# Gate and up columns of a SwiGLU block as one 2x2 block product, three of eight k units with seven products in place of eight

## The chip, the cores and the metric

The kernel runs on one core of a Trainium2 chip. The metric is the device time of one execution in microseconds (us); lower is better. The engines that matter here are TensorE (PE in the profile; its weight loads are PEld), VectorE (DVE), ScalarE (ACT), GpSimd (POOL) and SyncE (SP, which issues the weight DMAs).

## The reference, cut to what matters

One decoder layer on 256 tokens of width 2048, in float32: a SwiGLU half-step, a mixer, and a second SwiGLU half-step with its own weights. The change touches the two SwiGLU steps alone, and in them the first two products:

```python
D_MODEL, SEQ, D_FF = 2048, 256, 5504

def swiglu(x, w_gate, w_up, w_down):
    return (jax.nn.silu(x @ w_gate) * (x @ w_up)) @ w_down

f1 = swiglu(rms_norm(h, ffn1_pre_norm[l]), ffn1_w_gate[l], ffn1_w_up[l], ffn1_w_down[l])
h = h + 0.5 * rms_norm(f1, ffn1_post_norm[l])
...
f2 = swiglu(rms_norm(h, ffn2_pre_norm[l]), ffn2_w_gate[l], ffn2_w_up[l], ffn2_w_down[l])
h = h + 0.5 * rms_norm(f2, ffn2_post_norm[l])
```

## The kernel before, in words

Every product of float32 matrices is made of three matmuls on TensorE. A number is split into a high part that fits TensorE's short float32 form (`F32R`) and the rest: `split_into` (L135) writes `hi` with a ScalarE copy (L136) and `lo = src - hi` with a VectorE subtract (L137). `mm3` (L139) then issues hi*hi, lo*hi and hi*lo into one PSUM bank (L141, L142, L143). The normed tokens are kept split and transposed as `xhi`, `xlo`; the weights are split as they arrive.

The 256 tokens are two row tiles t = 0, 1 of 128. The 2048 rows of a weight matrix are 16 k tiles of 128. `D_FF` = 5504 columns are worked in blocks of `CB` = 512: ten of 512 and a last one of 384. The loop over the blocks is in `ffn` (L380). For each block, `gemm_block` (L145) makes gate, then `gemm_block` makes up. A `gemm_block` walks the eight pairs of k tiles; this text calls such a pair a **unit**. For each unit, `wload` (L114) brings a `raw` tile of 128 x 2 x 512 with one DMA on SP's queue, `wchunk` (L121) splits it into `whi` and `wlo`, and twelve matmuls follow (two row tiles, two k tiles, three each). So a unit of gate and up together takes 24 matmuls, and a block of 512 columns takes 192. `raw`, `whi` and `wlo` are rings of `RING` = 5 tiles each: ScalarE may split a new tile only when TensorE has finished with the one five tiles earlier.

Behind a block, ScalarE applies silu to gate (L411), `finish` (L394) multiplies it with up on VectorE into `hn` (L396), and one step later TensorE transposes `hn` (four 128x128 transposes per row tile, L206) and ScalarE copies the result to `hT` (L401) for the down projection. Such later steps are generators: `side.spawn` starts one, and each `side.pump()` in a gemm lets each go one step. PSUM has eight banks of 128x512 float32, handed out from one pool by `ps_tile`.

The program's statements aren't the order in which an engine gets its instructions: a list scheduler with the tile pools sets it when the kernel is built, and each engine then works its list in order. Splits of a later unit are therefore found ahead of work of an earlier one.

`rows` is a pool of eight 128x512 tiles for the norm weights that `load_bcast` (L189) loads in `out_proj`; `hkhi` and `hklo` (four buffers each) hold the split `hT` in the down projection.

Of the kernel before, what the change touches and what calls it, by code (L numbers as in the profile page):

```python
# [74 lines left out]
def kernel(ctx: ExitStack, tc: tile.TileContext, a: dict, out: bass.AP):  # L75
# [69 lines left out]
    def gemm_block(w_dram, c0, w, lhs, nkt=KT, held=None, raws=(), ready=()):  # L145
# [40 lines left out]
        return pss if nb > 1 else [ps[0] for ps in pss]  # L186


    def load_bcast(name, n, after):  # L189
# [4 lines left out]
        return t

# [184 lines left out]
    def ffn(pre, x, rs, post, pre_next, begin=None, ready=(), following=None):  # L380
        with ExitStack() as fctx:
# [22 lines left out]
            for f0 in range(0, DFF, CB):  # L404
                w = min(CB, DFF - f0)
                g = gemm_block(a[pre + "_w_gate"], f0, w, xl, held=None if f0 or begin else held,
                               raws=() if f0 else raws, ready=() if f0 else ready)
                s = []
                for t in range(NT):
                    st = fwork.tile([P, CB], F32, tag="silu", name=nm("silu"))  # L410
                    nc.scalar.activation(st[:, :w], g[t][:, :w], AF.Silu, scale=rs[t])  # L411
# [483 lines left out]
```

## Time and profile before

| | |
|---|---|
| median of 3 runs | 2181.24 us (2180.39 to 2182.26) |
| the profiled execution, its own time | 2182.85 us |
| its span, first to last instruction | 2181.1 us |
| granted TensorE clock, mean | 0.999 |
| TensorE busy | 2170.1 us, 99% |
| VectorE busy | 1163.3 us, 53% |
| ScalarE busy | 997.8 us, 46% |
| HBM read | 406.41 MB, 187 GB/s over the span |

The span is the part of the execution that the trace sees; 1.75 us of the execution's own time lie around it. A matmul's record runs from its start to the modelled end of its results, about 0.39 us for 512 columns, and the next one starts before that; what a matmul costs in a stream is the distance between starts. Rows of instructions read: line, engine, operation, output<-inputs, shape, count, then busy time and the mean of one, then the idle time before them and what ended it.

### The profile page before, as it was taken

The numbers are of one execution on the slowest core, as the hardware profiler recorded it, in microseconds if no ns is written. First come the engines' busy times: TensorE is split into PE (matmuls) and PEld (weight loads), VectorE is DVE, ScalarE is ACT, GpSimd is POOL, SyncE is SP. The second block draws the span as 40 slices with busy tenths as digits, with TensorE's granted clock in tenths as the row PEclk, the third lists the DMA queues.
The fourth block names the chain that finished last, engine by engine and source line by source line (L and its number), as shares of the span: only waits on it lengthen the run. The fifth ranks groups of instructions, "written<-read, shape, count | busy, mean of one in ns | idle before, by whom it ended". The sixth has DMA issues, their size and how long they took to land.

```text
span 2181.1 us, 26346 instructions
## 1 busy us (share of the span) xinstructions
PE 2170.1 (99%) x10204; PEld 1815.8 (83%) x10204; DVE 1163.3 (53%) x1277; ACT 997.8 (46%) x1227; POOL 34.3 (2%) x87
## 2 busy tenths in 40 slices
PE   9999999999999999999999999999999999999998
PEld 7888888898888888888888888888888888898887
DVE  5544454445555744657575556575444444445555
ACT  6444444444445564444434444464444444444443
POOL 0000000000000100000000000010000000000000
PEclk9999999999999999999999999999999999999999
DMA  7666666667667456655556775756666666576663
GB/s 259 188 190 188 191 192 185 192 179 238 193 194 227 146 175 193 174 149 143 161 157 179 200 207 187 226 190 182 187 192 192 184 192 190 170 225 193 194 194 129
DMA packets 189360, 410.24 MB, mean 188 GB/s; under 512 B 13697, under 2 KB 22305, under 8 KB 189234
## 3 DMA queue, kind: packets, MB, share of 16 engines
q1 hardware_dynamic: 183440, 399.69, 61.5%
q10 hardware_dynamic: 5794, 8.87, 1.2%
q8 instruction: 80, 1.31, 0.2%
q14 instruction: 46, 0.38, 0.0%
HBM read 406.41 MB, written 2.10 MB: 187 GB/s over the span
## 4 chain that ended last, share of the span: by engine, by line
PE 99%; DVE 0%; DMA 0%; ACT 0%; issue 0%; DVEq 0%; POOLq 0%; SPq 0%; POOL 0%; ACTq 0%
PE mm L141 23%; PE mm L143 23%; PE mm L142 23%; PE acc L142 8%; PE acc L141 8%; PE acc L143 8%; PE ps L206 2%; PE ps L568 1%; PE ps L618 0%; PE ps L575 0%; PE ps L552 0%; DMA raw<-in_ffn_w_gate_dram 0%; PE ps L621 0%; PE ps L628 0%; DVE wlo L137 0%; DVE h L331 0%
## 5 line engine op out<-in xcount | busy, mean ns | idle before, releaser
L137 DVE TENSOR_TENSOR wlo<-raw,whi 128x1024 fp32r<-128x1024 f32 (+3 forms) x740 | 896.7, 1213 | 921.7 <-ACT whi L136 881.0
L136 ACT ACTIVATE whi<-raw 128x1024 fp32r<-128x1024 f32 (+3 forms) x740 | 777.0, 1051 | 1083.1 <-PE mm L142 808.0
L141 PE MATMUL mm<-whi,xhi 128*128 128x512 f32 (+2 forms) x2120 | 819.0, 387 | 1.3 <-ACT xhi L265 1.2
L143 PE MATMUL mm<-wlo,xhi 128*128 128x512 f32 (+2 forms) x2120 | 812.4, 383 | 0.0
L142 PE MATMUL mm<-whi,xlo 128*128 128x512 f32 (+2 forms) x2120 | 812.2, 383 | 0.1
L141 PEld LDWEIGHTS mm<-whi,xhi 128*128 128x128 f32 x2120 | 398.5, 188 | 76.3 <-ACT xhi L265 2.4
L143 PEld LDWEIGHTS mm<-wlo,xhi 128*128 128x128 f32 x2120 | 398.3, 188 | 75.8
L142 PEld LDWEIGHTS mm<-whi,xlo 128*128 128x128 f32 x2120 | 398.5, 188 | 74.0 <-DVE xlo L137 0.4
L141 PE MATMUL acc<-whi,hkhi 128*128 128x512 f32 x640 | 249.2, 389 | 0.0
L143 PE MATMUL acc<-wlo,hkhi 128*128 128x512 f32 x640 | 249.0, 389 | 0.0
L142 PE MATMUL acc<-whi,hklo 128*128 128x512 f32 x640 | 249.0, 389 | 0.0
L143 PEld LDWEIGHTS acc<-wlo,hkhi 128*128 128x128 f32 x640 | 120.1, 188 | 24.9
L141 PEld LDWEIGHTS acc<-whi,hkhi 128*128 128x128 f32 x640 | 120.2, 188 | 24.9
L142 PEld LDWEIGHTS acc<-whi,hklo 128*128 128x128 f32 x640 | 120.1, 188 | 24.7
L141 PE MATMUL mm<-whi,oT 128*128 128x512 f32 x128 | 50.5, 395 | 0.0
L143 PE MATMUL mm<-wlo,oT 128*128 128x512 f32 x128 | 49.9, 390 | 0.0
L142 PE MATMUL mm<-whi,oT 128*128 128x512 f32 x128 | 49.8, 389 | 0.0
L141 PE MATMUL acc<-whi,xhi 128*128 128x512 f32 x100 | 39.1, 391 | 0.0
L143 PE MATMUL acc<-wlo,xhi 128*128 128x512 f32 x100 | 39.0, 390 | 0.0
L142 PE MATMUL acc<-whi,xlo 128*128 128x512 f32 x100 | 38.9, 389 | 0.0
L411 ACT ACTIVATE silu<-mm,r 128x512 f32<-128x512 f32 (+1 forms) x44 | 29.5, 670 | 13.9 <-PE mm L143 13.9
L137 DVE TENSOR_TENSOR held<-raw,held 128x512 fp32r<-128x512 f32 (+1 forms) x35 | 31.0, 915 | 7.3 <-ACT held L136 7.0
(191 smaller groups left out, 1052.7 us busy)
## 6 DMA issues: line engine op xcount, KB each, us to landing
raw<-in_ffn_w_down_dram SPq DMA_DIRECT2D x172, 512.0 KB, 4.6
raw<-in_w_in_dram SPq DMA_DIRECT2D x168, 512.0 KB, 3.9
raw<-in_ffn_w_up_dram SPq DMA_DIRECT2D x160, 512.0 KB, 3.6
raw<-in_ffn_w_gate_dram SPq DMA_DIRECT2D x159, 512.0 KB, 3.6
raw<-in_w_out_dram SPq DMA_DIRECT2D x32, 512.0 KB, 4.5
raw<-in_w_branch_gla_dram SPq DMA_DIRECT2D x16, 512.0 KB, 4.2
raw<-in_w_branch_hgrn_dram SPq DMA_DIRECT2D x16, 512.0 KB, 4.3
raw<-in_ffn_w_gate_dram SPq DMA_DIRECT2D x16, 384.0 KB, 3.4
```

The lines of the kernel that those rows point to most:

```text
L136: last[0] = nc.scalar.activation(hi, src, AF.Copy)
L137: nc.vector.tensor_tensor(lo, src, hi.bitcast(F32), op=ALU.subtract)
L141: nc.tensor.matmul(ps, lhsT=xhi, rhs=whi, start=start, stop=False)
L142: nc.tensor.matmul(ps, lhsT=xlo, rhs=whi, start=False, stop=False)
L143: nc.tensor.matmul(ps, lhsT=xhi, rhs=wlo, start=False, stop=stop)
L206: nc.tensor.transpose(dst_ps[:, i * P:(i + 1) * P], src[:, i * P:(i + 1) * P], ident)
L411: nc.scalar.activation(st[:, :w], g[t][:, :w], AF.Silu, scale=rs[t])
L568: nc.tensor.matmul(ps[:, i * 64:(i + 1) * 64], lhsT=kT[:, sl], rhs=halves(qT[:, sl])[1], start=True, stop=True)
```

## The change

The first block of each half-step stays as it was. For the ten others (nine of 512 columns and the one of 384), `gemm_pair` makes gate and up together, with four PSUM banks `c[t][i]` (t the row tile, i = 0 for gate and 1 for up). In the units 0, 1, 3, 5 and 7 it does the same 24 matmuls as before, gate first and then up. In the units 2, 4 and 6 (`SUMS`, here called **sum units**) it does the 2x2x2 block product (two row tiles, two k tiles, gate and up) with seven products in Winograd's form of Strassen's method, so 21 matmuls. Three of the products go straight to `c00`, `c01` and `c10`; four go to banks `p1`, `p5`, `p6`, `p7` of their own that run on over the three sum units.

The sums that this needs are made on VectorE. Of the tokens, once per half-step, by `operand_sums`: four sums of blocks for the three sum units together, split by ScalarE and VectorE, and kept in the `hkhi` and `hklo` buffers until the last block. Of the weights, in each sum unit: four adds of 128x512, then splits of the gate pair, of the changed up pair (`second`), of the pair `wsum`, and of a single 128x512 sum (`wall`). At a block's end five steps build `r00`, `r01`, `r10`, `r11` out of the four p banks (one ScalarE copy and four VectorE adds), and four VectorE adds put them into the c banks ahead of silu and `hn`. The splits of the next block's unit 0 are asked for ahead of these four. `rows` becomes four tiles of twice the size, which serve the sums in the gate and up part and the norm weights in the down projection.

Numbers of lines in the changed kernel differ: the split is L137 and L138 there, the three matmuls L142, L143 and L144, the added VectorE adds L248, the transposes L328, and `hn` L522.

On VectorE, in the stretch around the end of a block: before, where the third block of the first half-step ends (`wlo` are splits of the next units, `mm0` and `mm1` the PSUM banks of up).

```order
L137 TENSOR_TENSOR wlo_218_1247<-raw_216_1244,whi_217_1246 128x1024
L137 TENSOR_TENSOR wlo_221_1265<-raw_219_1262,whi_220_1264 128x1024
L396 SCALAR_TENSOR_TENSOR hn_204_1190<-mm0_177_1043,r_54_404,silu_175_1039 128x512
L396 SCALAR_TENSOR_TENSOR hn_205_1192<-mm1_178_1044,r_56_411,silu_176_1041 128x512
L137 TENSOR_TENSOR wlo_224_1283<-raw_222_1280,whi_223_1282 128x1024
L137 TENSOR_TENSOR wlo_227_1301<-raw_225_1298,whi_226_1300 128x1024
```

In the changed kernel at the same place (`wlo_268` is the split of the next block's unit 1 of gate, `wlo_271` that of up; the `psum` tiles hold r01 and, in turn, r10 and r11; the second `hn` is the row that follows the last one here):

```order
L138 TENSOR_TENSOR wlo_268_1361<-raw_266_1358,whi_267_1360 128x1024
L248 TENSOR_TENSOR psum_247_1262<-psum_247_1262,p6_208_1066 128x512
L248 TENSOR_TENSOR psum_248_1263<-psum_247_1262,p7_207_1065 128x512
L248 TENSOR_TENSOR wsum_276_1402<-raw_273_1396 128x512
L248 TENSOR_TENSOR psum_247_1262<-psum_247_1262,p5_206_1064 128x512
L248 TENSOR_TENSOR psum_248_1263<-psum_248_1263,p5_206_1064 128x512
L248 TENSOR_TENSOR c00_183_963<-c00_183_963,psum_247_1262 128x512
L248 TENSOR_TENSOR c10_185_965<-c10_185_965,psum_248_1263 128x512
L248 TENSOR_TENSOR c01_184_964<-c01_184_964,psum_247_1262 128x512
L138 TENSOR_TENSOR wlo_271_1379<-raw_269_1376,whi_270_1378 128x1024
L248 TENSOR_TENSOR c11_186_966<-c11_186_966,psum_248_1263 128x512
L522 SCALAR_TENSOR_TENSOR hn_258_1314<-c01_184_964,r_54_404,silu_255_1309 128x512
```

Where two rows of `hn` stood among splits, nine adds and a split now stand between the last early split and the first `hn`.

On VectorE inside the fourth block, before: a run of splits and nothing else.

```order
L137 TENSOR_TENSOR wlo_230_1319<-raw_228_1316,whi_229_1318 128x1024
L137 TENSOR_TENSOR wlo_233_1337<-raw_231_1334,whi_232_1336 128x1024
L137 TENSOR_TENSOR wlo_240_1361<-raw_238_1358,whi_239_1360 128x1024
L137 TENSOR_TENSOR wlo_243_1379<-raw_241_1376,whi_242_1378 128x1024
L137 TENSOR_TENSOR wlo_246_1397<-raw_244_1394,whi_245_1396 128x1024
```

In the changed kernel, at the sum unit 6 (`wlo_307` is unit 5 of up, `wlo_320` unit 7 of gate):

```order
L248 TENSOR_TENSOR wsum_312_1568<-raw_309_1562 128x512
L248 TENSOR_TENSOR raw_309_1562<-raw_309_1562,raw_308_1560 128x512
L138 TENSOR_TENSOR wlo_307_1545<-raw_305_1542,whi_306_1544 128x1024
L248 TENSOR_TENSOR wsum_312_1568<-raw_309_1562 128x512
L138 TENSOR_TENSOR wlo_311_1565<-raw_308_1560,whi_310_1564 128x1024
L248 TENSOR_TENSOR raw_308_1560<-raw_308_1560,wsum_312_1568 128x512
L138 TENSOR_TENSOR wlo_314_1573<-raw_309_1562,whi_313_1572 128x1024
L138 TENSOR_TENSOR wlo_320_1608<-raw_318_1605,whi_319_1607 128x1024
L138 TENSOR_TENSOR wsumh_316_1577<-wsum_312_1568,wsumh_315_1576 128x1024
L138 TENSOR_TENSOR wall_317_1581<-raw_308_1560,wall_317_1581 128x512
```

The unit's own rows are four adds, three splits of 1024 and one of 512; splits of the units beside it stand between them.

On TensorE at the start of the fourth block, before: the last matmuls of unit 0 of gate, then both groups of transposes.

```order
L142 MATMUL mm1_207_1195<-whi_209_1198,xlo1_4_100 128x512
L143 MATMUL mm1_207_1195<-wlo_210_1199,xhi1_3_99 128x512
L206 MATMUL ps_211_1214<-ident_91,hn_204_1190 128x128 x4
L206 MATMUL ps_212_1220<-ident_91,hn_205_1192 128x128 x4
L141 MATMUL mm0_206_1194<-whi_214_1228,xhi0_1_97 128x512
L142 MATMUL mm0_206_1194<-whi_214_1228,xlo0_2_98 128x512
```

In the changed kernel at the same place:

```order
L143 MATMUL c10_262_1320<-whi_250_1295,xlo1_4_100 128x512
L144 MATMUL c10_262_1320<-wlo_251_1296,xhi1_3_99 128x512
L328 MATMUL ps_264_1334<-ident_91,hn_258_1314 128x128 x4
L142 MATMUL c00_260_1318<-whi_267_1360,xhi0_1_97 128x512
L328 MATMUL ps_265_1340<-ident_91,hn_259_1316 128x128 x4
L142 MATMUL c01_261_1319<-whi_253_1301,xhi0_1_97 128x512
L143 MATMUL c01_261_1319<-whi_253_1301,xlo0_2_98 128x512
```

The transposes still stand behind twelve matmuls of the new block, and one matmul has moved between the two groups.

The diff, cut to its core:

```diff
+SUMS = (2, 4, 6)
...
-    rows = ctx.enter_context(tc.tile_pool(name="rows", bufs=8))
+    rows = ctx.enter_context(tc.tile_pool(name="rows", bufs=4))
...
+    def operand_sums(x, new_part, out):
...
+        for t in range(NT):
+            ab.append(views("ab", 2))
+            for i in range(2):
+                nc.vector.tensor_tensor(ab[t][i], x[0][t][:, sl[i], :].bitcast(F32),
+                                        x[1][t][:, sl[i], :].bitcast(F32), op=ALU.add)
+            yield
+        (a11, a12), (a21, a22) = ab
+        (d, s2), (s4, s3) = views("sums", 2), views("sums", 2)
+        nc.vector.tensor_tensor(d, a22, a21, op=ALU.subtract)
+        nc.vector.scalar_tensor_tensor(s2, d, -1.0, a11, op0=ALU.mult, op1=ALU.subtract)
+        yield
+        nc.vector.tensor_tensor(s3, a11, a21, op=ALU.subtract)
+        nc.vector.tensor_tensor(s4, a12, s2, op=ALU.add)
+        for name, s in (("d", d), ("s2", s2), ("s3", s3), ("s4", s4)):
+            yield
...
+            split_into(hi, lo, s)
+            out[name] = hi, lo
+
+    def gemm_pair(ws, c0, w, lhs, sums, ready):
+        c = [[ps_tile(f"c{t}{i}") for i in range(2)] for t in range(NT)]
...
+        for u in range(nu):
+            k0 = 2 * u
+            last_sum = u == SUMS[-1]
+            if u not in SUMS:
+                if u or not ready:
+                    ready = [split(0, k0)] + ([split(1, k0)] if u == nu - 1 else [])
+                if u == nu - 1:
...
+                    nc.scalar.copy(r00, p1)
+                    add(r01, r00, p6)
+                    add(r10, r01, p7)
+                    add(r01, r01, p5)
+                    add(r11, r10, p5)
+                for i in range(2):
+                    parts = ready.pop(0) if ready else split(i, k0)
+                    for t in range(NT):
+                        for j in range(2):
+                            product(c[t][i], lhs(t, k0 + j), parts[j], (t, i),
+                                    u == nu - 1 and j == 1)
+                    side.pump()
+                continue
+            (ra, _), (rb, _) = load(0, k0), load(1, k0)
+            first = wchunk(None, w, raw=(ra, False))
+            wsum = row_tile("wsum")[:, :, :w]
+            add(wsum[:, 0, :], rb[:, 1, :], rb[:, 0, :])
+            add(rb[:, 0, :], rb[:, 0, :], ra[:, 0, :])
+            add(wsum[:, 1, :], rb[:, 0, :], rb[:, 1, :])
+            second = wchunk(None, w, raw=(rb, False))
+            hi, lo = [row_tile("wsumh", F32R)[:, :, :w] for _ in range(2)]
+            add(ra[:, 1, :], ra[:, 1, :], wsum[:, 1, :])
+            split_into(hi, lo, wsum)
+            allp = row_tile("wall", F32R)[:, :, :w]
+            split_into(allp[:, 0, :], allp[:, 1, :], ra[:, 1, :])
...
+            product(p["p1"], lhs(0, k0), first[0], "p1", last_sum)
+            product(c[0][0], lhs(0, k0 + 1), first[1], (0, 0))
+            product(c[0][1], part("s4", u), second[1], (0, 1))
+            side.pump()
+            product(p["p5"], part("d", u), second[0], "p5", last_sum)
+            product(p["p7"], part("s3", u), (hi[:, 0, :], lo[:, 0, :]), "p7", last_sum)
+            product(p["p6"], part("s2", u), (hi[:, 1, :], lo[:, 1, :]), "p6", last_sum)
+            product(c[1][0], lhs(1, k0 + 1), (allp[:, 0, :], allp[:, 1, :]), (1, 0))
+            side.pump()
+        c1 = c0 + w
+        if c1 < DFF:
+            ready = [split(i, 0, c1, min(CB, DFF - c1)) for i in range(2)]
+        for (t, i), x, op in (((0, 0), r00, ALU.add), ((1, 0), r10, ALU.add),
+                              ((0, 1), r01, ALU.subtract), ((1, 1), r11, ALU.subtract)):
+            add(c[t][i][:, :w], c[t][i][:, :w], x, op)
...
+    def row_tile(s, dt=F32):
+        return rows.tile([P, 2, CB], dt, tag="row", name=nm(s))
...
-                g = gemm_block(a[pre + "_w_gate"], f0, w, xl, held=None if f0 or begin else held,
-                               raws=() if f0 else raws, ready=() if f0 else ready)
+                if f0:
+                    g, u, ready = gemm_pair((a[pre + "_w_gate"], a[pre + "_w_up"]), f0, w, xl,
+                                            sums, ready)
+                else:
+                    g = gemm_block(a[pre + "_w_gate"], f0, w, xl, held=None if begin else held,
+                                   raws=raws, ready=ready)
+                    ready = ()
...
-                u = gemm_block(a[pre + "_w_up"], f0, w, xl)
+                if not f0:
+                    side.spawn(operand_sums(x, new_part, sums))
+                    u = gemm_block(a[pre + "_w_up"], f0, w, xl)
```

More of the change, by code (lines that the diff above doesn't have):

```diff
@@ L186, in gemm_block, with views @@
         return pss if nb > 1 else [ps[0] for ps in pss]
-    def load_bcast(name, n, after):
-        t = rows.tile([P, CB], F32, tag="row", name=nm("row"))
+    def operand_sums(x, new_part, out):
+        yield
+        sl = [slice(2 * SUMS[0] + i, None, 2 * (SUMS[1] - SUMS[0])) for i in range(2)]
+        n = len(SUMS)
+        def views(s, m):
+            t = row_tile(s).rearrange("p i c -> p (i c)")
+            return [t[:, i * n * P:(i + 1) * n * P].rearrange("p (k c) -> p k c", c=P)
+                    for i in range(m)]
+        ab = []
+        for t in range(NT):
[12 more added lines that the diff above has]
+        for name, s in (("d", d), ("s2", s2), ("s3", s3), ("s4", s4)):
+            yield
+            hi, lo = [new_part(i).rearrange("p i c -> p (i c)")[:, :n * P]
+                      .rearrange("p (k c) -> p k c", c=P) for i in range(2)]
+            split_into(hi, lo, s)
+            out[name] = hi, lo
@@ new lines, in gemm_pair, with part, product, load @@
+    def gemm_pair(ws, c0, w, lhs, sums, ready):
+        c = [[ps_tile(f"c{t}{i}") for i in range(2)] for t in range(NT)]
+        p = {}
+        begun = set()
+        nu = KT // 2
+        def part(name, u):
+            hi, lo = sums[name]
+            i = SUMS.index(u)
+            return hi[:, i, :], lo[:, i, :]
+        def product(ps, x, wp, key, stop=False):
+            mm3(ps[:, :w], x, wp, key not in begun, stop)
+            begun.add(key)
+        def load(i, k0, c0=c0, w=w):
+            return wload(ws[i][k0 * P:(k0 + 2) * P, c0:c0 + w].rearrange("(k p) c -> p k c", p=P), w)
+        def split(i, k0, c0=c0, w=w):
+            return wchunk(None, w, raw=load(i, k0, c0, w))
+        def add(o, x, y, op=ALU.add):
+            nc.vector.tensor_tensor(o, x, y, op=op)
+        for u in range(nu):
[5 more added lines that the diff above has]
+                if u == nu - 1:
+                    p1, p5, p6, p7 = [p[s][:, :w] for s in ("p1", "p5", "p6", "p7")]
+                    t0, t1 = row_tile("psum"), row_tile("psum")
+                    r00, r01, r10, r11 = [t[:, i, :w] for t in (t0, t1) for i in range(2)]
+                    nc.scalar.copy(r00, p1)
[23 more added lines that the diff above has]
+            split_into(allp[:, 0, :], allp[:, 1, :], ra[:, 1, :])
+            if not p:
+                for name in ("p1", "p5", "p7", "p6"):
+                    p[name] = ps_tile(name)
+            product(p["p1"], lhs(0, k0), first[0], "p1", last_sum)
[13 more added lines that the diff above has]
+            add(c[t][i][:, :w], c[t][i][:, :w], x, op)
+        return *[[c[t][i] for t in range(NT)] for i in range(2)], ready
@@ L317, in out_proj @@
                 if name is not None:
-                    row.append(load_bcast(name, i % 4 + 2 & 3, last[0]))
+                    load_bcast(row, name, i % 4 + 2 & 3, last[0])
             for t in range(NT):
@@ L391, in ffn, with new_part @@
             xl = lhs_of(x)
-            hT = []
+            hT, sums = [], {}
+            def new_part(i):
+                s = ("hkhi", "hklo")[i]
+                return fwork.tile([P, 2, NT * P], F32R, tag=s, name=nm(s), bufs=4)
             def finish(t, f0, w, u, s):
```

10 lines of the change are left out of this document (6 added, 4 removed).

## The prediction

> **What bounds the kernel now.** I read the profile's page first: busy shares, shares by slice, and the chain that ended last.
>
> ```profile
> PE 2170.1 (99%) x10204; PEld 1815.8 (83%) x10204; DVE 1163.3 (53%) x1277; ACT 997.8 (46%) x1227; POOL 34.3 (2%) x87
> ...
> PE   9999999999999999999999999999999999999998
> PEclk9999999999999999999999999999999999999999
> ...
> PE 99%; DVE 0%; DMA 0%; ACT 0%; issue 0%; DVEq 0%; POOLq 0%; SPq 0%; POOL 0%; ACTq 0%
> ```
>
> TensorE is busy without a hole at full clock, and the chain that ended last is TensorE alone. Fewer matmuls shorten the kernel as long as the others keep up. So two questions follow: what is a matmul worth, and does VectorE, which gets the new work, keep up. For the first, the chain in order of time has the transposes of two blocks in a row, and the timeline of TensorE shows the 384-wide block up to the first matmul of the down projection, and twelve matmuls of that projection:
>
> ```profile
> 105.07 0.87 PE ps L206 x8
> 149.49 0.87 PE ps L206 x8
> ...
> 486.09 0.33 PE L141 MATMUL mm<-whi,xhi 128*128 128x384 f32 x1
> ...
> 491.81 0.39 PE L141 MATMUL acc<-whi,hkhi 128*128 128x512 f32 x1
> ...
> 599.98 0.39 PE L141 MATMUL acc<-whi,hkhi 128*128 128x512 f32 x1
> ...
> 602.70 0.39 PE L141 MATMUL acc<-whi,hkhi 128*128 128x512 f32 x1
> ```
>
> A block takes 149.49 - 105.07 = 44.42 us: 0.87 for the transposes and 43.55 for 192 matmuls, 0.2268 each. At 384 columns 33 matmuls lie between the two quoted starts: 5.72 / 33 = 0.173.
>
> For the second, the table of stages for that block, and who waits in it:
>
> ```profile
> 105.07:149.49 44.42, 44.42 (x202) 36.88 (x201) 22.29 (x20) 20.37 (x23) 0.00 (x0) 1.00 0.66 190
> ...
> ACT whi L136 <- PE mm L142: 25.1, 17, 1.7
> DVE wlo L137 <- ACT whi L136: 20.1, 14, 1.5
> ```
>
> TensorE works all 44.42 us, VectorE 22.29 and ScalarE 20.37. ScalarE waits 25.1 us for TensorE to give `whi` buffers back, and VectorE waits behind ScalarE: both are ahead as far as their five buffers let them.
>
> **The change part by part.**
>
> *Matmuls removed.* A sum unit has 21 in place of 24; three sum units in a block save nine. Over two half-steps: 18 blocks of 512 save 162 x 0.2268 = 36.7 us and two of 384 save 18 x 0.173 = 3.1. Together 39.9 us, all on the path. In the instruction order, TensorE's list is 180 rows shorter. A block becomes 44.42 - 2.04 = 42.38 us. In a sum unit every third matmul goes to another bank. The down projection does that already, and its twelve matmuls from 599.98 to 602.70 take 0.2267 each, so nothing is added for it.
>
> The Trainium skill ("TensorE: Matmul & The Clock Gate", section "Back-to-back issue gap") gives an isolated matmul of N columns a gap of N/2.4 + 2.5 ns, 216 for 512; the trace has 227, so the trace decides. By that figure the saving would be an estimated 37.9 us.
>
> *VectorE, work per block.* The prices:
>
> ```profile
> L137 DVE TENSOR_TENSOR wlo<-raw,whi 128x1024 fp32r<-128x1024 f32 x698 | 854.8, 1226 | 871.2 <-ACT whi L136 830.5 <-PE ps L206 36.0 <-PE ps L552 1.5
> ...
> L396 DVE SCALAR_TENSOR_TENSOR hn<-mm,r,silu 128x512 f32<-128x512 f32 x40 | 29.4, 748 | 1.0 <-PE mm L143 0.9
> L137 DVE TENSOR_TENSOR hklo<-hT,hkhi 128x512 fp32r<-128x512 f32 x42 | 28.4, 685 | 1.6 <-ACT hkhi L136 1.6
> ...
> L372 DVE TENSOR_TENSOR acc<-acc,row 128x512 f32<-128x512 f32 x24 | 16.7, 697 | 25.6 <-ACT sq L252 25.6
> ...
> L347 DVE TENSOR_TENSOR u<-h,row 128x512 f32<-128x512 f32 x16 | 10.6, 684 | 0.1
> ...
> 100.53 1.23 DVE L137 TENSOR_TENSOR wlo<-raw,whi 128x1024 fp32r<-128x1024 f32 x1 [1.49 <-ACT whi L136]
> 101.67 1.46 DVE L396 SCALAR_TENSOR_TENSOR hn<-mm,r,silu 128x512 f32<-128x512 f32 x2
> 103.25 1.23 DVE L137 TENSOR_TENSOR wlo<-raw,whi 128x1024 fp32r<-128x1024 f32 x1
> ...
> 890.21 0.75 DVE L523 SCALAR_TENSOR_TENSOR go<-mm,r,go 128x512 f32<-128x512 f32 x1
> 891.00 0.69 DVE L529 TENSOR_TENSOR go<-go,gnorm 128x512 f32<-128x512 f32 x1
> ```
>
> An add between SBUF tiles costs like `u`, 684 ns; one with a PSUM operand like `acc`, 697; a split of 1024 costs 1226 and of 512 costs 685. A sum unit adds one split of 1024, one of 512 and four adds: 1.226 + 0.685 + 4 x 0.684 = 4.65 us, three of them 13.9. The block's end adds eight adds of 0.697 = 5.6. The block had 22.29, of which two `hklo` splits (2 x 0.685) belong to the down projection: 20.9. The sum is 40.4 us against 42.38. That is the upper end, since an instruction behind another starts before its end: the split at 100.53 would end at 101.76, and `hn` starts at 101.67. So 0.085 comes off for each of some 30 rows that stand back to back. A row that needs the one just ahead of it loses that: `go` at 891.00 starts 0.04 behind the end of 890.21, 0.12 later than otherwise; a block has about four such. That gives 40.4 - 2.6 + 0.5 = 38.3 us, which I take, by the two starts just shown. VectorE goes from half full to 90%, and TensorE keeps the longer list.
>
> The Trainium skill ("VectorE: DVE Perf Modes", section "The DRAIN you can't avoid") says that the next operation cannot issue until the pipe of the last one is empty, a rule against many small VectorE rows such as these. The starts at 100.53 and 101.67 speak against it here; what it would make of the time is the third rival.
>
> *VectorE, the chain at a block's end.* Here the sum doesn't decide, but one wait does: twelve matmuls into the next block TensorE needs the first `hn`. I set T = 0 at the start of that block. The row ahead of the adds, the split of the next block's unit 1 of gate, needs the buffers of unit 6 of up, which `p5` reads last. That is 33 matmuls ahead of T, so -7.5; the `whi` buffer is free one matmul earlier, and the matmul's results end 0.39 behind its start: -7.5 again. ScalarE's split:
>
> ```profile
> L136 ACT ACTIVATE whi<-raw 128x1024 fp32r<-128x1024 f32 x698 | 740.0, 1061 | 1034.6 <-PE mm L142 762.2 <-PE acc L142 249.7 <-issue 9.0
> L411 ACT ACTIVATE silu<-mm,r 128x512 f32<-128x512 f32 x40 | 27.2, 680 | 13.2 <-PE mm L143 13.1
> ```
>
> It ends at -6.4, VectorE's part at -5.3. `p6` is whole at -6.0, so r01 starts at -5.3. Then eight adds at 0.61 (one at 0.60) and 0.12 for r10: -0.3. The split of unit 1 of up, 1.14: 0.9. The add to `c11`, whose last matmul ends at 0.16: 1.5. The two `hn` at 0.72: 2.2 and 2.9. TensorE asks for the first at 12 x 0.2268 = 2.72 and, four transposes (0.44) and one matmul later, for the second at 3.38. So both are there, with 0.5 us to spare. It is the tightest place of the change. Silu on `c00` (0.68) falls at -1.5 to -0.8 and hides.
>
> *VectorE, inside the block.* Behind the second `hn` a row with two waits starts 0.12 late (103.25 behind 101.67 + 1.46). Then unit 2's gate split ends at 4.2, its three adds at 6.2, the split of `second` at 7.4, of `wsum` at 8.5 and of `wall` at about 9.2; TensorE begins unit 2 at 48 x 0.2268 + 0.87 = 11.8. From there the buffers pace VectorE: unit 4's `wsumh` waits until `p7` and `p6` of unit 2 have read theirs (15.8), 6 us ahead of TensorE's unit 4 (22.0). No wait of TensorE there.
>
> *ScalarE.* A copy of 512 costs
>
> ```profile
> L136 ACT ACTIVATE hkhi<-hT 128x512 fp32r<-128x512 f32 x42 | 25.5, 615 | 0.1
> ```
>
> so a block has 20.37, less 2 x 0.62 for `hkhi`, plus 3 x (1.06 + 0.62) for the sum units and 0.6 for r00: 24.8 us of 42.4, hidden.
>
> *Token sums.* Twelve VectorE rows of 384 per half-step, each at most like this `hn` of 384:
>
> ```profile
> L396 DVE SCALAR_TENSOR_TENSOR hn<-mm,r,silu 128x384 f32<-128x384 f32 x4 | 2.3, 611 | 0.0
> ```
>
> That is 12 x 0.61 = 7.3 us, in the first block's up half, where VectorE is half idle (22.29 of 44.42). Hidden; without that cover 15 us for both half-steps.
>
> *DMAs.* The same bytes on the same queue, 190 GB/s becoming 199. A sum unit holds two of the five `raw` tiles until its last split, so a load for the next sum unit starts when unit 2's `second` is split (7.4) and takes
>
> ```profile
> raw<-in_ffn_w_up_dram SPq DMA_DIRECT2D x160, 512.0 KB, 3.6
> ```
>
> to 11.0; VectorE asks for it behind unit 3's splits, at about 11.5. No loss, or some tenths that the 6 us above cover. The row tiles hold norm weights again only in the down projection, behind the last sums: nothing.
>
> *Down projection.* `hkhi` and `hklo` come free with the last block's unit 6, 27 matmuls of 0.173 = 4.7 us ahead of the first down matmul; a split takes 0.62 + 0.69. Hidden.
>
> **The sum.** The profiled execution took 2182.85 us, its span is 2181.1; 2182.85 - 39.9 = 2143.0. It lies 1.6 above the median of the runs, so the median becomes 2181.24 - 39.9 = 2141.3. Its own range, with half a us per half-step for edges on either side and up to 0.2 per block at the tight place, is 2139 to 2146.
>
> **The rivals.**
>
> 1. *The `hn` come late.* The chain above has thirteen rows and 0.5 us to spare. For: every wait between engines that I set to nothing counts here in full. Against: `hn` waited only 1.0 us in total before. At 1 us late per block, over 20 blocks, 20 us come back: 2161; between 0.3 and 1.9 us late, 2147 to 2179.
>
> 2. *VectorE becomes the bound: slower.* Each of the three wide splits of a sum unit needs ScalarE's copy first, and two of those wait for an add. If VectorE stood through ScalarE's 1.06 us each time, 9 x 1.06 = 9.5 us, a block would take 38.3 + 9.5 = 47.8, which is 3.4 more than before: 20 x 3.4 = 68, or 2249. It decides from 44.42 - 38.3 = 6.1 us of standing per block. For: VectorE waits 20.1 us per block for ScalarE now. Against: that is ScalarE waiting for buffers, and in the new order a split or add of another unit stands between nearly every ScalarE copy and its use.
>
> 3. *No overlap between VectorE's rows.* Then the block holds 40.9 us of work, still under 42.38, but the twelve rows from r01 to the second `hn` take 0.085 more each: 1.0 late, 0.5 past the slack, 20 x 0.5 = 10: 2151. By the Trainium skill's rule on the DRAIN ("VectorE: DVE Perf Modes", the section named above) it would go this way. The starts quoted above speak against it.
>
> That TensorE might not get fewer matmuls is out: the order shows 180 rows less.
>
> **How the numbers follow.** Forecast 0.60; late `hn` 0.23; no overlap 0.03; VectorE as the bound 0.09; 0.05 for something between, near no change. A difference of 0.2%, about 4 us, is what a measurement of this kernel can tell. Faster: 0.60 + 0.22 + 0.03 = 0.85. Slower: 0.09 + 0.02 = 0.11. The same: 0.04. The range takes in the forecast's own, the third rival and the larger part of the first: 2138 to 2165.
>
> **What would show it right or wrong.** Right: 42.4 us between the transposes of neighbouring blocks, TensorE still at 99%, VectorE near 38 us per block, no wait of the transposes for `hn`. Late `hn` would show as TensorE idle ahead of the transposes with VectorE as the releaser. VectorE as the bound would show as matmuls of sum units waiting for `wsumh` or `wall`, and TensorE well under 99% in gate and up. If the 180 matmuls are gone, TensorE has no idle time and the block is still longer than 42.4, the price of a matmul is wrong.

## The result, and the profile after

The changed kernel takes 2143.96 us (median of 4 runs, 2142.88 to 2144.19) against 2181.24 (4 runs, 2180.39 to 2182.26): a ratio of 0.9828, with an interval of 0.9811 to 0.9845. The profiled execution took 2143.80 us, its span is 2142.0.

The page of the changed kernel, its busy times, VectorE's and TensorE's shares by slice, and the chain that ended last:

```profile
PE 2130.2 (99%) x10024; PEld 1781.7 (83%) x10024; DVE 1506.8 (70%) x1821; ACT 1101.6 (51%) x1375; POOL 34.6 (2%) x87
...
PE   9999999999999999999999999999999999999998
...
DVE  6889899885455754657575556577889998975455
...
PE 98%; DMA 1%; DVE 1%; ACT 0%; issue 0%; DVEq 0%; POOLq 0%; POOL 0%; ACTq 0%
```

TensorE has 180 matmuls fewer and is still full; VectorE has gone from 53% to 70% of the span, and to eight or nine tenths where gate and up are made. What is new is one per cent each for a DMA and VectorE in the chain that ended last. The table of stages for three blocks (start and end are those of the transposes; then length, and busy time of TensorE, its weight loads, VectorE, ScalarE and GpSimd, each with its count of instructions; then the granted clock, the DMA engines' busy share and GB/s):

```profile
102.67:145.58 42.91, 42.56 (x193) 35.03 (x191) 37.50 (x45) 24.35 (x27) 0.00 (x0) 1.00 0.62 195
145.58:188.02 42.44, 42.44 (x191) 35.21 (x192) 38.40 (x46) 24.37 (x27) 0.00 (x0) 1.00 0.65 199
1572.74:1615.15 42.41, 42.41 (x193) 35.15 (x192) 38.04 (x46) 24.46 (x27) 0.00 (x0) 1.00 0.63 199
```

A block is 42.4 us long in place of 44.4, VectorE works 38.0 us of it and ScalarE 24.4. One block of these is 0.5 longer. VectorE's timeline at its end shows why:

```profile
137.08 1.40 DVE L248 TENSOR_TENSOR psum<-psum,p 128x512 f32<-128x512 f32 x2
139.45 0.69 DVE L248 TENSOR_TENSOR wsum<-raw 128x512 f32<-128x512 f32 x1 [0.97 <-DMA raw<-in_ffn_w_up_dram]
140.06 1.28 DVE L248 TENSOR_TENSOR psum<-psum,p 128x512 f32<-128x512 f32 x2
141.25 1.89 DVE L248 TENSOR_TENSOR c<-c,psum 128x512 f32<-128x512 f32 x3
143.05 1.22 DVE L138 TENSOR_TENSOR wlo<-raw,whi 128x1024 fp32r<-128x1024 f32 x1
144.18 0.69 DVE L248 TENSOR_TENSOR c<-c,psum 128x512 f32<-128x512 f32 x1
144.78 1.40 DVE L522 SCALAR_TENSOR_TENSOR hn<-c,r,silu 128x512 f32<-128x512 f32 x2
```

The `wsum` row is the first weight add of the next block's unit 2. It stands in the middle of the row of adds that leads to `hn`, and here it waits 0.97 us for its load, which the chain of waits has as

```profile
134.51 4.91 DMA raw<-in_ffn_w_up_dram
```

4.9 us from issue to landing. Everything behind it is late, so TensorE's transposes wait (first row); at the next block's end, where the load is in time, they don't (second row). This is TensorE's timeline:

```profile
145.58 0.66 PE L328 MATMUL ps<-ident,hn 128*128 128x128 f32 x4 [0.35 <-DVE hn L522]
...
188.02 0.60 PE L328 MATMUL ps<-ident,hn 128*128 128x128 f32 x4
```

There `hn` is early, in VectorE's timeline of the same block end:

```profile
186.67 1.40 DVE L522 SCALAR_TENSOR_TENSOR hn<-c,r,silu 128x512 f32<-128x512 f32 x2
```

The first of the two ends at about 187.4 (186.67 and half of 1.40), 0.6 us ahead of the transposes. In the whole trace such waits come to

```profile
PE ps L328 <- DVE hn L522: 0.7, 2, 0.4
```

two of them, of 0.35 us or so each. TensorE loses 0.5 us at each: the first of its transposes starts 0.74 us behind the matmul ahead of it (144.84 to 145.58), where matmuls in a stream start 0.23 apart. The other 16 block ends that have such an add in the row (18 in all) had their load in time, but not by much: in the trace it landed after 3.1 to 3.8 us, and 0.1 to 0.8 us ahead of the add.

### The profile page after: what moved, and what is told of

It reads as the page before. It is cut to its first block, busy times and chain, and to the rows that moved or that the text cites. A ratio compares the mean times of both kernels' runs of the same rounds, so it can differ in the third digit from the quotient of the medians.

```text
span 2142.0 us, 27066 instructions
## 1 busy us (share of the span) xinstructions
PE 2130.2 (99%) x10024; PEld 1781.7 (83%) x10024; DVE 1506.8 (70%) x1821; ACT 1101.6 (51%) x1375; POOL 34.6 (2%) x87
## 4 chain that ended last, share of the span: by engine, by line
PE 98%; DMA 1%; DVE 1%; ACT 0%; issue 0%; DVEq 0%; POOLq 0%; POOL 0%; ACTq 0%
PE mm L142 10%; PE mm L144 10%; PE mm L143 10%; PE c L143 10%; PE c L142 10%; PE c L144 10%; PE acc L142 9%; PE acc L143 9%; PE acc L144 9%; PE p L144 2%; PE p L143 2%; PE p L142 2%; PE ps L328 2%; PE ps L700 1%; DMA raw<-in_ffn_w_up_dram 0%; PE ps L750 0%
## 5 line engine op out<-in xcount | busy, mean ns | idle before, releaser
L138 DVE TENSOR_TENSOR wlo<-raw,whi 128x1024 fp32r<-128x1024 f32 (+3 forms) x740 | 892.8, 1211 | 524.0 <-ACT whi L137 509.7
L137 ACT ACTIVATE whi<-raw 128x1024 fp32r<-128x1024 f32 (+3 forms) x740 | 777.4, 1051 | 891.9 <-PE mm L143 321.2
L142 PE MATMUL c<-whi,xhi 128*128 128x512 f32 (+1 forms) x860 | 333.0, 387 | 0.0
L144 PE MATMUL c<-wlo,xhi 128*128 128x512 f32 (+1 forms) x860 | 330.1, 384 | 0.0
L143 PE MATMUL c<-whi,xlo 128*128 128x512 f32 (+1 forms) x860 | 330.0, 384 | 0.0
L142 PE MATMUL mm<-whi,xhi 128*128 128x512 f32 (+1 forms) x840 | 326.4, 389 | 1.3 <-ACT xhi L387 1.2
L143 PE MATMUL mm<-whi,xlo 128*128 128x512 f32 (+1 forms) x840 | 321.0, 383 | 0.0
L144 PE MATMUL mm<-wlo,xhi 128*128 128x512 f32 (+1 forms) x840 | 321.0, 383 | 0.0
L142 PE MATMUL acc<-whi,hkhi 128*128 128x512 f32 x640 | 249.2, 389 | 0.0
L144 PE MATMUL acc<-wlo,hkhi 128*128 128x512 f32 x640 | 249.0, 389 | 0.0
L143 PE MATMUL acc<-whi,hklo 128*128 128x512 f32 x640 | 249.0, 389 | 0.0
L144 PEld LDWEIGHTS c<-wlo,xhi 128*128 128x128 f32 x860 | 161.4, 188 | 30.1
L143 PEld LDWEIGHTS c<-whi,xlo 128*128 128x128 f32 x860 | 161.5, 188 | 29.8
L142 PEld LDWEIGHTS c<-whi,xhi 128*128 128x128 f32 x860 | 161.5, 188 | 29.1
L142 PEld LDWEIGHTS mm<-whi,xhi 128*128 128x128 f32 x840 | 158.2, 188 | 31.9 <-ACT xhi L387 2.5
L144 PEld LDWEIGHTS mm<-wlo,xhi 128*128 128x128 f32 x840 | 158.0, 188 | 30.5
L143 PEld LDWEIGHTS mm<-whi,xlo 128*128 128x128 f32 x840 | 158.1, 188 | 29.5 <-issue 0.2
L144 PEld LDWEIGHTS acc<-wlo,hkhi 128*128 128x128 f32 x640 | 120.1, 188 | 25.1
L142 PEld LDWEIGHTS acc<-whi,hkhi 128*128 128x128 f32 x640 | 120.2, 188 | 24.8
L143 PEld LDWEIGHTS acc<-whi,hklo 128*128 128x128 f32 x640 | 120.2, 188 | 24.6
L248 DVE TENSOR_TENSOR wsum<-raw 128x512 f32<-128x512 f32 (+1 forms) x120 | 81.0, 675 | 16.0 <-DMA raw<-in_ffn_w_up_dram 15.0
L138 DVE TENSOR_TENSOR wsumh<-wsum,wsumh 128x1024 fp32r<-128x1024 f32 (+1 forms) x60 | 71.5, 1192 | 0.0
```

Of the source, the lines that this page charges most:

```text
L137: last[0] = nc.scalar.activation(hi, src, AF.Copy)
L138: nc.vector.tensor_tensor(lo, src, hi.bitcast(F32), op=ALU.subtract)
L142: nc.tensor.matmul(ps, lhsT=xhi, rhs=whi, start=start, stop=False)
L143: nc.tensor.matmul(ps, lhsT=xlo, rhs=whi, start=False, stop=False)
L144: nc.tensor.matmul(ps, lhsT=xhi, rhs=wlo, start=False, stop=stop)
L248: nc.vector.tensor_tensor(o, x, y, op=op)
```

## The experiments

Theory T: the time is TensorE's matmuls at 0.2268 us each; VectorE is hidden as long as each result is there when TensorE asks, and the tightest such place is the row of adds at a block's end. The rivals differ by run. "Order set by hand" is the edit of e2, which is kept where it is named.

### e1: the pairing without the sums

```diff
-            if u not in SUMS:
+            if True:
...
-                if u == nu - 1:
+                if False:
...
-            add(c[t][i][:, :w], c[t][i][:, :w], x, op)
...
-                    side.spawn(operand_sums(x, new_part, sums))
```

> Gate and up are worked block by block together and in the new order, but every unit keeps its eight products (24 matmuls), and there are no sums, neither of weights nor of x nor at a block's end. Theory T (the saving is the 180 matmuls removed at 0.2268 us, and nothing else of the change counts): back to the time before, 2181 to 2184 us, blocks 44.4 us apart. Rival L (the gain comes from working gate and up together, fewer stage ends or better order, and not from the matmuls): 2144 to 2165 us.

2182.27 us (2181.21 to 2182.85, 10 runs), ratio 1.0001 (0.9992 to 1.0011). Working gate and up together is worth nothing; rival L is out. Two blocks of it in the table of stages:

```profile
104.38:193.24 88.86, 88.86 (x401) 73.73 (x400) 43.34 (x38) 39.58 (x43) 0.00 (x0) 1.00 0.66 190
```

### e2: the order set by hand

```diff
+                            with tc.issue_after(last_tp[0].ins):
                                 product(c[t][i], lhs(t, k0 + j), parts[j], (t, i),
...
-            first = wchunk(None, w, raw=(ra, False))
-            wsum = row_tile("wsum")[:, :, :w]
-            add(wsum[:, 0, :], rb[:, 1, :], rb[:, 0, :])
+            with tc.issue_after(last_hn[0].ins):
+                first = wchunk(None, w, raw=(ra, False))
+                wsum = row_tile("wsum")[:, :, :w]
+                add(wsum[:, 0, :], rb[:, 1, :], rb[:, 0, :])
```

> All of the change is kept; only the order is set by hand: on VectorE unit 2's first split and its first weight add stand behind the second hn in place of ahead of the chain's end, and on TensorE the transposes keep their place. Theory T: the chain at a block's end gets about 0.6 us more room, the two waits of the transposes (0.47 us each, behind the add that waits for its DMA) go, every pair of neighbouring blocks is 42.4 us apart: 2143 us, 1 us less than the changed kernel at most. Rival W (something later in VectorE's row becomes late when the add goes behind hn, since unit 2's preparation ends 0.6 to 1.9 us later): waits at unit 2, 2144 to 2160 us.

`last_hn[0]` and `last_tp[0]` are the last `hn` and the last transpose that the program has made; `tc.issue_after` puts the rows of the same engine that stand in it behind that one.

2141.95 us (2141.48 to 2142.26, 4 runs), ratio 0.9817 (0.9802 to 0.9831). That is 2.0 us under the changed kernel; the intervals of the two ratios overlap, the runs themselves don't. Both waits of the transposes are gone, which is 1.0 of the 2.0; the rest I don't account for. Two blocks, where e1 has 88.86:

```profile
102.62:187.40 84.78, 84.78 (x384) 70.35 (x382) 76.16 (x89) 48.48 (x54) 0.00 (x0) 1.00 0.64 199
```

4.08 us for 18 matmuls is 0.2267 each.

### e3 and e4: four more adds, at two places

Both have the order set by hand and four more adds of 512 columns per block. In e3 they stand in the row at a block's end:

```diff
             add(c[t][i][:, :w], c[t][i][:, :w], x, op)
+            if (t, i) == (0, 1):
+                for more in (ALU.add, ALU.subtract) * 2:
+                    add(c[t][i][:, :w], c[t][i][:, :w], r00, more)
```

> As the run with the order set by hand, with four more VectorE adds of 512 columns (PSUM and SBUF, plus and minus the same row twice) in the chain between p6 and the first hn, about 2.6 us per block. Theory T (VectorE's work in sum is hidden, but the chain at a block's end has about 1.1 us of room, and each us past it comes to the path): 1.5 us per block of the path, 20 blocks, 25 to 35 us more than without them, 2168 to 2180 us, with the transposes waiting for hn in every block. Rival V (VectorE's sum per block is what counts; 38.0 + 2.6 = 40.6 us is still under 42.4): no change, 2142 to 2146 us.

In e4 they stand in unit 3:

```diff
-                    ready = [split(0, k0)] + ([split(1, k0)] if u == nu - 1 else [])
+                    raw = load(0, k0)
+                    if u == 3:
+                        for more in (ALU.add, ALU.subtract) * 2:
+                            add(raw[0][:, 0, :], raw[0][:, 0, :], raw[0][:, 1, :], more)
+                    ready = [wchunk(None, w, raw=raw)] + ([split(1, k0)] if u == nu - 1 else [])
```

> As the run with the order set by hand, with four more VectorE adds of 512 columns in unit 3, in the middle of the block, about 2.6 us per block; the weight they touch is added and taken away again twice. Theory T (in the middle of a block VectorE is about 6 us ahead, so 2.6 us more are hidden): within 2 us of the run without them, 2142 to 2146 us. Rival V2 (VectorE at 90% of a block is already the limit, so that any add is paid in full): 20 x 2.6 = 52 us more, 2195 us.

At the block's end: 2183.92 us (2182.13 to 2186.64, 10 runs), ratio 1.0011 (1.0002 to 1.0021), 42.0 us over e2. In unit 3: 2142.80 us (2141.85 to 2143.26, 4 runs), ratio 0.9820 (0.9804 to 0.9836), 0.85 over e2, where the two sets of runs overlap. The table of stages for a block of e3, and then of e4:

```profile
148.42:192.98 44.56, 42.84 (x192) 35.09 (x192) 40.85 (x49) 24.12 (x27) 0.00 (x0) 1.00 0.59 189
```

```profile
145.22:187.62 42.40, 42.40 (x192) 35.18 (x191) 40.17 (x49) 24.02 (x27) 0.00 (x0) 1.00 0.64 198
```

VectorE's work in a block is nearly the same; the place decides. In e3 VectorE's timeline has the six adds ahead of `hn`, then TensorE's has the transposes waiting:

```profile
188.05 4.09 DVE L248 TENSOR_TENSOR c<-c,psum 128x512 f32<-128x512 f32 x6
192.17 1.41 DVE L527 SCALAR_TENSOR_TENSOR hn<-c,r,silu 128x512 f32<-128x512 f32 x2
```

```profile
192.98 1.20 PE L332 MATMUL ps<-ident,hn 128*128 128x128 f32 x7 [1.72 <-DVE hn L527]
```

In e2 this row of VectorE has two adds in 1.29 us:

```profile
184.34 1.29 DVE L248 TENSOR_TENSOR c<-c,psum 128x512 f32<-128x512 f32 x2
```

so the four are 2.80 us, and 20 blocks pay 42.0 / 20 = 2.10 of it on average: 0.7 were covered. Theory T holds; its number (25 to 35) was low, since an add that needs the one ahead of it costs 0.70 and not 0.65, and since the room was 0.7 and not 1.1. Rival V is out at this size, and V2 as well: VectorE at 40.2 us of 42.4 is hidden.

### e5: all the sums, and 24 matmuls again

```diff
             product(p["p1"], lhs(0, k0), first[0], "p1", last_sum)
+            product(p["p1"], lhs(1, k0), first[0], "p1")
```

> The changed kernel with its sums, with one product too many in each sum unit (a second row half against the first gate part, added into p1, so the output is another): 24 matmuls per sum unit again, all of VectorE's and ScalarE's new work kept. Theory T (time is the number of matmuls on TensorE): 39.9 us more than the changed kernel, 2182 to 2185 us. Rival V (VectorE's and ScalarE's rows set the length of a block as much as TensorE): the extra matmuls fall partly into time in which TensorE would stand, 2144 to 2170 us.

2182.24 us (2181.26 to 2183.98, 10 runs), ratio 1.0003 (0.9993 to 1.0012), 38.3 over the changed kernel. With VectorE's new work kept, the matmuls alone bring the whole time back, as T says.

### e6: four sum units, 1, 2, 4 and 6

```diff
-SUMS = (2, 4, 6)
+SUMS = (1, 2, 4, 6)
```

> Four of the eight units with seven products (unit 1 too), everything else as in the changed kernel. TensorE's list is 60 matmuls shorter, 18 x 3 x 0.2268 + 2 x 3 x 0.173 = 13.3 us. VectorE's work per block goes from 38.0 to about 42.3 us, against 41.7 of TensorE. Theory T (VectorE now is the bound, and the row at a block's end has less room, since unit 1's sums stand in it): no further gain, blocks of 42.4 to 43 us, 2143 to 2160 us, with TensorE waiting for VectorE in every block. Rival M (the time follows the matmuls as long as VectorE is nearly hidden): 2131 us.

2147.47 us (2146.59 to 2149.59, 4 runs), ratio 0.9846 (0.9831 to 0.9862): 60 matmuls fewer and no faster. The table of stages for the second and the eighth such block of the first half-step:

```profile
101.12:142.82 41.70, 41.70 (x190) 34.61 (x189) 40.92 (x50) 22.77 (x27) 0.00 (x0) 1.00 0.63 202
354.36:396.84 42.48, 42.04 (x190) 34.44 (x189) 42.06 (x51) 24.58 (x29) 0.00 (x0) 1.00 0.62 198
```

The first two blocks of a half-step take the 41.7 us of TensorE's list. Then VectorE's lead is used up and it works 42.06 of 42.48 us. From the fifth such block on, TensorE waits in each block at the second sum unit, for ScalarE's split of `second`; that split starts as an add on VectorE ends, behind rows that VectorE has worked one after the other, without a wait, since 351.65. The timelines of VectorE, ScalarE and TensorE have it so:

```profile
362.80 0.69 DVE L250 TENSOR_TENSOR raw<-raw,raw 128x512 f32<-128x512 f32 x1
...
363.57 1.06 ACT L137 ACTIVATE whi<-raw 128x1024 fp32r<-128x1024 f32 x1 [3.31 <-issue]
...
364.68 0.50 PE L142 MATMUL c<-whi,hkhi 128*128 128x512 f32 x1 [0.44 <-ACT whi L137]
```

Here VectorE sets the length, as T says. But that is only about half of what e6 misses against M (2147.47 against 2131). From the tenth block on, the last block and the down projection take 2.6 and 5.9 us more than in the changed kernel in the two half-steps. The waits of the whole run that belong to this are those for `hn` and `silu` of the last block, where the down projection starts:

```profile
PE c L142 <- ACT whi L137: 5.3, 12, 0.5
PE ps L330 <- DVE hn L524: 3.7, 4, 1.9
PE acc L142 <- ACT silu L544: 1.5, 2, 1.1
```

The first row is the wait in the blocks, the other two lie in the tail; about 3 us of the 8.5 there are not in these rows and stay open.

### e7 and e8: weight adds on GpSimd

e7 is e6 with this edit, e8 the changed kernel with it:

```diff
-            add(wsum[:, 0, :], rb[:, 1, :], rb[:, 0, :])
+            nc.gpsimd.tensor_tensor(wsum[:, 0, :], rb[:, 1, :], rb[:, 0, :], op=ALU.add)
...
-            add(wsum[:, 1, :], rb[:, 0, :], rb[:, 1, :])
+            nc.gpsimd.tensor_tensor(wsum[:, 1, :], rb[:, 0, :], rb[:, 1, :], op=ALU.add)
```

> Four units with seven products, and the two weight adds of each sum unit moved to GpSimd, which has no work in these stages. VectorE has 8 x 0.69 = 5.5 us less per block than with four units on VectorE: about 37 us against TensorE's 41.7. No trace here shows an add on GpSimd of this size. Theory T (VectorE's row at the end of the block decides): 2131 to 2140 us if a GpSimd add takes under about 2 us, since unit 1 now needs its sums early; if it takes more, the wait for unit 1's sums comes to the path, 1 us late per block being 20 us: 2140 to 2175 us. Rival M (the matmuls alone): 2131 us in any case.

> The changed kernel with the two weight adds of each sum unit on GpSimd. VectorE has 6 x 0.69 = 4.1 us less per block, and the first of these adds no longer stands in VectorE's row at a block's end. Theory T (VectorE is hidden but for the two DMA waits): 2142 to 2144 us; the two waits of the transposes go. Rival G (GpSimd's adds are slow, or slow VectorE's down while they run, so that a sum unit comes late): 2150 to 2200 us, with TensorE waiting for wsumh or wall.

e7: 2184.54 us (2182.37 to 2187.34, 10 runs), ratio 1.0015 (1.0006 to 1.0025). e8: 2179.07 us (2175.35 to 2183.75, 10 runs), ratio 0.9990 (0.9980 to 1.0000). e7 lies past the ranges that I gave. Its TensorE waits above all in sum units, for VectorE's split of `wsum`, and less for `hn`:

```profile
PE p L144 <- DVE wsumh L138: 31.6, 18, 2.0
PE ps L330 <- DVE hn L524: 9.1, 14, 1.1
```

In e8 I was wrong to expect that the waits go. The time falls into rival G's range, but not by G's wait (for `wsumh` or `wall`). VectorE has less to do (35.7 us of a block from 326.37 to 370.39), yet TensorE waits for `hn` at nearly every block's end:

```profile
PE ps L328 <- DVE hn L522: 27.0, 19, 2.0
```

The new order of e8 has the unit's second add in the row at the block's end, and that one waits for GpSimd's, which waits for a load. GpSimd's timeline, then VectorE's:

```profile
362.94 1.29 POOL L277 TENSOR_TENSOR wsum<-raw 128x512 f32<-128x512 f32 x1 [14.53 <-DMA raw<-in_ffn_w_up_dram]
```

```profile
364.26 0.69 DVE L248 TENSOR_TENSOR raw<-raw,raw 128x512 f32<-128x512 f32 x1 [2.01 <-POOL wsum L277]
```

It is the wait that e2 took away, made longer and put into nearly every block.

### e9 and e10: four sum units away from the block's end

e9 has the order set by hand, and e10 is e9 with the last weight add on GpSimd:

```diff
-SUMS = (2, 4, 6)
+SUMS = (2, 3, 5, 6)
...
-            add(ra[:, 1, :], ra[:, 1, :], wsum[:, 1, :])
+            nc.gpsimd.tensor_tensor(ra[:, 1, :], ra[:, 1, :], wsum[:, 1, :], op=ALU.add)
```

> The order set by hand as before, and four units with seven products, placed as units 2, 3, 5 and 6, so that none stands right behind a block's end. 60 matmuls fewer than in the changed kernel, 13.3 us; VectorE's work per block about 42 us against TensorE's 41.7. Theory T (VectorE's sum per block now sets the block): neighbouring blocks 42.0 to 42.5 us apart once VectorE's lead is used up, 2136 to 2148 us, with TensorE waiting in sum units. Rival C (with four units it was only unit 1's place behind the block's end that held TensorE up): 41.7 us apart, 2128 to 2131 us.

> As the run with units 2, 3, 5 and 6, with the last weight add of each sum unit on GpSimd: 4 x 0.61 = 2.4 us less on VectorE per block. In the run with GpSimd adds, VectorE's wide splits took 1.27 us on average in place of 1.22, and 2.32 where a GpSimd add lay beside. Theory T: VectorE falls to about 40 to 41 us per block if a GpSimd add costs it 0.3 us on average, blocks 41.7 us apart, 2128 to 2134 us. Rival G (each GpSimd add takes as much from VectorE as it gives, 0.6 to 1.1 us, or brings wall too late): 42 to 43 us per block, 2136 to 2160 us.

e9: 2149.28 us (2147.95 to 2150.39, 4 runs), ratio 0.9848 (0.9830 to 0.9866), 1 us above T's range, and T's place was wrong too: in most blocks it is the transposes that wait, behind a row at the block's end that is late. A block in the table of stages, and the transposes at its end:

```profile
355.60:397.94 42.34, 42.14 (x189) 34.52 (x189) 41.93 (x51) 24.80 (x29) 0.00 (x0) 1.00 0.63 199
```

```profile
397.94 0.66 PE L331 MATMUL ps<-ident,hn 128*128 128x128 f32 x4 [0.20 <-DVE hn L526]
```

VectorE is at 41.9 of 42.3, so rival C is out for the blocks. As in e6, the tail counts too: from its first matmul to its last the down projection takes 241.1 and 240.4 us in the two half-steps, against 235.9 and 234.4 in the changed kernel, 11 of the 21 us that e9 lies above rival C's 2128. e10: 2211.05 us (2210.36 to 2211.27, 4 runs), ratio 1.0132 (1.0116 to 1.0149), slower than before the change and far past what either theory gave. TensorE's wait at a sum unit of it, and all such waits:

```profile
231.21 0.50 PE L144 MATMUL p<-wsumh,hkhi 128*128 128x512 f32 x1 [1.99 <-DVE wsumh L138]
...
PE p L144 <- DVE wsumh L138: 50.5, 38, 2.0
```

How much of this is the order that the scheduler made for it, and how much GpSimd, these runs don't separate.

### e11: GpSimd in the middle of the block

e2 with the edit of e10 to the last weight add, and three sum units.

> The order set by hand, three sum units as in the changed kernel, and the last weight add of each sum unit on GpSimd; nothing of it stands in the row at a block's end. Theory T (in the middle of the block some us are to spare, and what GpSimd adds cost is only seen in VectorE's row): 2141 to 2144 us, VectorE's wide splits longer where a GpSimd add lies beside them. Rival G (a GpSimd add of 1.3 to 2.2 us makes wall late for the last product of the unit): TensorE waits ahead of c10 of a sum unit, 2145 to 2180 us.

2141.92 us (2141.84 to 2142.07, 4 runs), ratio 0.9816 (0.9799 to 0.9834): as e2, as T says, and rival G is out here. But VectorE didn't get less to do. The groups of VectorE's wide splits in e2 and then in e11, and e11's page:

```profile
L138 DVE TENSOR_TENSOR wlo<-raw,whi 128x1024 fp32r<-128x1024 f32 x698 | 851.3, 1223 | 509.6 <-ACT whi L137 497.0 <-PE ps L329 8.9 <-PE ps L686 1.5
```

```profile
L138 DVE TENSOR_TENSOR wlo<-raw,whi 128x1024 fp32r<-128x1024 f32 x698 | 900.6, 1298 | 501.6 <-ACT whi L137 486.9 <-PE ps L329 9.2 <-PE ps L686 1.5
```

```profile
PE 2128.3 (99%) x10024; PEld 1781.3 (83%) x10024; DVE 1525.4 (71%) x1761; ACT 1099.0 (51%) x1375; POOL 144.7 (7%) x147
```

Sixty adds left VectorE (about 40 us at 0.69 and less), and the splits took 49.3 us more: its busy time rose from 1508.6 us in e2 to 1525.4. Unlike in e8 and e10, the slower rows still end before TensorE asks for them (it has no wait for `hn`, `wsumh` or `wall`), so nothing shows in the time.

### e12: four sum units in every second block

The order set by hand, `SUMS = (1, 2, 4, 6)`, and

```diff
-            if u not in SUMS:
+            if u not in SUMS or u == 1 and c0 // CB % 2 == 0:
```

> The order set by hand, and four units with seven products (1, 2, 4, 6) in every second block, three (2, 4, 6) in the others: the 512-wide blocks with four are five in each half-step. That is 10 x 3 = 30 matmuls fewer than with three in every block, 30 x 0.2268 = 6.8 us. VectorE has about 42 us of work in a block of 41.7, then 38 us in one of 42.4, so 80 in 84.1. Theory T (VectorE's sum has to fit over some blocks, since it can work ahead, and the row at a block's end has to be in time; in the run with units 1, 2, 4 and 6 in every block the first two blocks were 41.7 us apart): blocks 41.7 and 42.4 us in turn, 2135 to 2138 us. Rival C (a four-unit block is late at its second sum unit whatever comes before it): 0.3 to 0.8 us per such block come back, 2138 to 2144 us.

2138.72 us (2138.38 to 2139.35, 5 runs), ratio 0.9802 (0.9789 to 0.9816): the fastest kernel here, 5.2 us under the changed one. Two blocks of it:

```profile
101.42:143.80 42.38, 42.38 (x192) 35.17 (x191) 38.76 (x45) 21.54 (x25) 0.00 (x0) 1.00 0.62 199
143.80:185.95 42.15, 42.15 (x189) 34.41 (x188) 41.57 (x51) 26.48 (x31) 0.00 (x0) 1.00 0.62 199
```

The block with four takes 42.15 and not 41.7: 0.45 each comes back, and with it 4.5 of the 6.8 us would; the medians have 3.6 of it back (2138.72 against 2141.95 - 6.8 = 2135.2). So rival C came here and T's full gain did not. The 80.3 us of VectorE do fit into the 84.5 us of two blocks, but within the block with four, unit 2 comes too soon behind unit 1. VectorE's split of its `second`, and the matmul of TensorE that needs it, in the two timelines:

```profile
153.54 1.22 DVE L138 TENSOR_TENSOR wlo<-raw,whi 128x1024 fp32r<-128x1024 f32 x1
```

```profile
154.81 0.50 PE L144 MATMUL c<-wlo,hkhi 128*128 128x512 f32 x1
```

The matmul starts as the split ends, 0.32 us behind the one ahead of it (154.49), and the next one 0.34 behind it (155.15), where matmuls here are usually 0.227 apart: 0.2 of the 0.45 us are lost there; the rest stays open. Whether the order set by hand is at fault there (it holds unit 1's first rows back behind `hn`; without it, in e6, the first two blocks took 41.7) wasn't tried.

## Why the prediction was right, point by point

- **The price of a matmul.** Forecast 0.2268 and 39.9 us in all. Measured 0.2267 in e1 against e2, and 2182.27 - 2141.95 = 40.3 us. The estimate of 37.9 us, from the Trainium skill's figure for an isolated matmul ("TensorE: Matmul & The Clock Gate", section "Back-to-back issue gap"), is 2.4 us short of that: in this stream of split float32 matmuls they start 227 ns apart. That the changed kernel's own saving, 2181.24 - 2143.96 = 37.3, comes near it is chance, since the waits and the median of before (last point) are in it.
- **The block.** Forecast 42.38, measured 42.39 in e2 and 42.41 and 42.44 in the quoted undisturbed blocks.
- **VectorE and ScalarE per block.** Forecast 38.3 and 24.8, measured 38.0 and 24.4. The second rival (VectorE as the bound) didn't come, and e4 shows that it wouldn't have at 40.2 us either; e6 shows where it begins.
- **Rows behind one another.** Three adds in 1.89 us, where one alone takes 0.69, are 0.60 apart. So the third rival is out. The prediction quoted the rule behind it by half: the Trainium skill ("VectorE: DVE Perf Modes", section "The DRAIN you can't avoid") adds in the same place that a next operation that is not held starts earlier, and these rows agree with that. The loss of a row that needs the one ahead shows in e3: 0.70 apart.
- **The tightest place.** Forecast: the first `hn` 0.5 us early. Measured: 0.6. That it is the tight place e3 shows, where 2.80 us more cost 2.10 in each of 20 blocks, while the same work elsewhere (e4) cost 0.04.
- **The step that failed: DMAs.** "No loss, or some tenths that the 6 us above cover." I had followed the loads to the rows inside the block, where there are 6 us, but one add that needs such a load stands in the row of 0.5 us: `wsum` of unit 2, which the order showed. I gave it 0.61 for its time and nothing for its wait; the only landing that I worked out, at the median of 3.6 us, was that of a later unit's load. At two of the 18 block ends with such an add the load took 4.9, which cost 1.0 us in all. By its mechanism this is the first rival, at two places. That it was not more is in part luck: at the other 16 the load was 0.1 to 0.8 us early, a margin that the forecast had not worked out.
- **The sum.** For the profiled execution 2143.0 was forecast and 2143.80 measured; the two waits explain that. The median came out at 2143.96, 2.7 above 2141.3. Part of this is the base: 2181.24 came from a few runs, and the kernel before gave medians of 2181.92 to 2182.19 beside the experiments. From 2181.93 (19 runs, beside e1 to e4) the forecast saving leads to 2142.0, which e2, without the two waits, meets with 2141.95. The changed kernel lies 1.9 above that; the waits are 1.0 of it, and the rest is open.

## What to carry to other kernels

Count an engine's new work twice: its sum per block against the engine that bounds, and every row between the last result it needs and the next one the bounding engine asks for. Four adds per block cost 42.0 us in all at one place, and 0.85 at most at another. A row that waits for a load has no business in that stretch: put it behind, by hand if a scheduler decides. When work is traded between engines up to the bound, a part of the places (every second block) can still pay when all of them no longer do.

## What the hardware showed that was not expected

A GpSimd add beside a VectorE split holds the split up. The timelines of GpSimd and then of VectorE in e11:

```profile
189.90 1.29 POOL L283 TENSOR_TENSOR raw<-raw,wsum 128x512 f32<-128x512 f32 x1 [21.22 <-DVE wsum L248]
199.60 2.15 POOL L283 TENSOR_TENSOR raw<-raw,wsum 128x512 f32<-128x512 f32 x1 [8.41 <-DMA raw<-in_ffn_w_up_dram]
```

```profile
190.12 2.15 DVE L138 TENSOR_TENSOR wlo<-raw,whi 128x1024 fp32r<-128x1024 f32 x1 [0.45 <-ACT whi L137]
192.19 1.21 DVE L138 TENSOR_TENSOR wsumh<-wsum,wsumh 128x1024 fp32r<-128x1024 f32 x1
```

The split that starts 0.22 us behind the GpSimd add takes 2.15 us, while the next one takes 1.21: it ends 1.1 us behind the add's end at 191.19, about its own length, as if it had begun there. Other adds of GpSimd's take 2.15 us in place of 1.29. The Trainium skill ("SBUF — State Buffer", section "SBUF: two separate sides") says that the two engines share a pair of ports as an exclusive lock, which a VectorE operation with two SBUF inputs takes too when the GpSimd operation reads SBUF, and that whoever comes second waits for the whole instruction. The rows agree. So each of the 54 adds of 512 columns that were moved, 0.69 us long, cost VectorE's splits 0.91 us (49.3 / 54).
